# A fused decoder block: sums of the turned input on GpSimd, bias transfers and the fourth conv tile at other places

## The chip, the cores and the metric

The kernel runs on one core of a Trainium2 chip. A core has five engines that run their own instruction streams and wait for each other by semaphores: TensorE (PE, matmuls, with its weight loads PEld), VectorE (DVE), ScalarE (ACT), GpSimd (POOL) and SyncE (SP, here an issuer of DMA transfers). Matmuls write into PSUM, the other data lies in SBUF; both have 128 partitions. The metric is the time of one execution on the device in microseconds (us), lower is better.

## The reference

One decoder layer over 1024 tokens of width 1024, in fp32 throughout. A normalised input feeds one wide projection, whose columns are q, k, v, u and g. Two mixers work side by side, differential attention over q, k, v and a causal depthwise convolution of width 31 over a gated u; their results are merged by gates and projected, and a feed-forward part follows.

```python
h = rms_norm(x, attn_norm_w)
q, k, v, u, g = split(h @ w_in)                  # 1024, 1024, 1024, 2048, 2048 columns
q, k = rms_norm(q, q_norm_w), rms_norm(k, k_norm_w)      # per head half of 64
s = q_i @ k_i.T * 64**-0.5 + bias[rel]           # 8 heads, i = 1, 2; causal
a = (softmax(s_1) - lam * softmax(s_2)) @ v
y_a = rms_norm(a, subln_w) * (1 - lam_init) @ w_proj_attn
u_a, u_b = split(u)
c = causal_conv31(u_a * sigmoid(u_b), conv_w) + conv_b
y_b = silu(layer_norm(c)) @ w_proj_conv
g_a, g_b = split(sigmoid(g + gate_b))
x = x + (g_a * y_a + g_b * y_b) @ w_out
gt, up = split(rms_norm(x, ffn_norm_w) @ w_gate_up)
out = x + (silu(gt) * up) @ w_down
```

`bias[rel]` is a table of 32 buckets by 8 heads, looked up by the distance of query and key.

## The kernel before, in words

An fp32 matmul is made of three matmuls of a shorter type. Each operand is split into a high part (`hi`, a rounding cast on ScalarE, `split_hi`, L120) and a low part (`lo`, the operand less its high part, on VectorE, `split_lo`, L125, or on GpSimd, L131, while `low_by_pool` is set), and hi by hi, lo by hi and hi by lo are summed in PSUM (L168 to L170, and L944 in the products of the U stage).

The first stage is written as a generator. It yields a few dozen times, and the loop around it, at the bottom of the kernel, counts the yields in `n` and places background work at them. Its parts, in order:

- The opening (to 66.6 us). The 1024 tokens are normalised 128 at a time (`norm`, its last step L695 on VectorE) and turned by TensorE (L705, into PSUM as `px`) into `hT_hi` and `hT_lo`, the transposed input in two parts. Between the turns stand the first matmuls of V0 and of the first half of u. The steps are written in an order that is kept.
- The V stage: V1 and V2, two items of 256 columns of v, each in four steps of 48 matmuls, 256 wide. While they run, GpSimd, VectorE and ScalarE make the sums of the turned input that the next part needs.
- The U stage: u in seven pairs of column blocks (`u_pair`, c = 1 to 7). A pair is computed with seven products of 12 matmuls, 512 wide, in place of eight (a Strassen form over a 2 x 2 split of the contraction and of the tokens). The operands on the side of the input, T1 to T4, are sums of quarters F of the input; they are made once, in `sums_of_h`: F = hi + lo (`add`, on GpSimd, two instructions of 128x1024 for each quarter), differences of quarters (`less` and `less4`, on VectorE), and their high and low parts (`parts`, low on GpSimd, L890). The operands on the side of the weights are sums made for each pair in `prepare` (`s12`, `s34`, on GpSimd, L926 to L929), with their splits and that of the block 22 (`sh`, `sl`).
- Q0 and V3 (`run(last)`), and then the attention, whose first scores are L1243.

`tsum` is the list of the steps of `sums_of_h`; three are taken at each step of the V stage. `ws.fetch` loads weights ahead.

Two kinds of work run beside it. The convolution is 31 taps on VectorE for each of eight channel tiles (L580; ScalarE does the first tap, L574). Four tiles sum in a PSUM buffer of which there is one, so a tile ends with a copy to SBUF by ScalarE (`done`, L584) before the next begins; all four must be through before the attention takes that PSUM space. `bg` holds the taps as a list, `bg.step` issues some at each yield (2.75 on average), and `bg.until` issues what is due at a point. The bias is made by `bias_rows` at n = 18, 19, 20 (one matmul each, a copy by ScalarE into a `u2` tile, a transfer `b_d` on GpSimd's queue) and `bias_skew`, eight transfers on GpSimd's queue that spread a row over 128 partitions (`t_d<-b_d`, 576 KB each), one for each head.

Instructions are placed by a scheduler on their engine's stream in an order that may differ from that of the code, except where `after(...)` or `in_order` binds them; each engine and each DMA queue then runs its stream in order.

## Time and profile before

| | us |
|---|---|
| median of 3 runs | 1770.57 |
| lowest, highest | 1767.92, 1772.21 |
| the profiled execution | 1767.17 |
| its span | 1765.4 |
| TensorE busy | 1735.8 (98% of the span) |
| VectorE busy | 1267.4 (72%) |
| ScalarE busy | 856.5 (49%) |
| GpSimd busy | 198.7 (11%) |
| mean granted clock of TensorE | 0.994 of full speed |

The span is what lies between the first and the last instruction of the profiled execution. "Busy" counts the time in which an engine worked on an instruction; waiting is not in it. GpSimd's work lies almost all in the first stage. A row of the timeline has the start, the duration, the engine, the line, the operation, output and inputs by their names, the tile's shape, a count, and in brackets the idle time ahead of it with what ended that (`[2.29 <-DVE u L125]`: 2.29 us idle, released by VectorE's line 125). A row of a group has count, busy time and mean ns of one, and the idle time ahead. L12 is line 12 of the kernel before.

### The profile page before, as it was taken

How to read it: one execution, taken by the hardware profiler on the slowest of the kernel's cores; microseconds unless marked ns; L12 is line 12 of the kernel's file. 1: busy time of each engine (PE TensorE's matmuls, PEld its weight loads, DVE VectorE, ACT ScalarE, POOL GpSimd, SP SyncE). 2: the span in 40 equal slices, each digit the busy share in tenths (PEclk: the TensorE clock that was granted, in tenths of full speed). 3: DMA queues.
4: the chain of work that ended last, by engine and by line, in shares of the span. 5: the costliest groups of instructions: out<-in, count | busy, mean ns of one | idle time of the engine just before them, and what ended most of it. 6: DMA issues, size and time to landing. Idle time of an engine off the chain costs nothing.

```text
span 1765.4 us, 25829 instructions
## 1 busy us (share of the span) xinstructions
PE 1735.8 (98%) x9293; PEld 1493.0 (85%) x9293; DVE 1267.4 (72%) x2098; ACT 856.5 (49%) x1952; POOL 198.7 (11%) x190
## 2 busy tenths in 40 slices
PE   9989999999999999999999999999999999999999
PEld 7987789899998998987788788888888888888887
DVE  7696687799888988979678534877667666565544
ACT  5233335667776776755457313643333333333332
POOL 2696771000000000000000000000000000000000
PEclk9999999999999999999999999999999999999999
DMA  6235434433443433334773444234554544498663
GB/s 203 84 126 182 133 96 138 138 91 108 126 120 97 143 102 120 116 106 127 273 269 121 161 169 147 90 102 143 165 163 153 172 154 148 163 344 304 214 216 131
DMA packets 253253, 271.68 MB, mean 154 GB/s; under 512 B 15746, under 2 KB 177602, under 8 KB 253124
## 3 DMA queue, kind: packets, MB, share of 16 engines
q1 hardware_dynamic: 250848, 263.25, 46.0%
q0 software_dynamic: 1840, 5.19, 1.1%
q8 instruction: 73, 1.20, 0.3%
q10 hardware_dynamic: 436, 1.58, 0.2%
q14 instruction: 56, 0.46, 0.1%
HBM read 175.55 MB, written 78.16 MB: 144 GB/s over the span
## 4 chain that ended last, share of the span: by engine, by line
PE 88%; DVE 4%; ACT 2%; DMA 2%; POOL 2%; issue 1%; SPq 0%; ACTq 0%; DVEq 0%; POOLq 0%
PE acc L944 29%; PE acc L498 12%; PE pg L168 10%; PE pg L169 10%; PE pg L170 10%; PE sc L1243 2%; PE sc L1244 2%; PE pT L1282 2%; PE wo L168 2%; PE wo L170 2%; PE wo L169 2%; POOL F L864 1%; PE pW L169 1%; PE pW L168 1%; PE pW L170 1%
## 5 line engine op out<-in xcount | busy, mean ns | idle before, releaser
L580 DVE SCALAR_TENSOR_TENSOR acc<-u,cw,acc 128x1023 f32<-128x1023 f32 (+14 forms) x240 | 303.8, 1266 | 7.9 <-ACT acc L574 4.8
L168 PE MATMUL pg<-whi,hT_hi 128*128 128x256 f32 x704 | 200.7, 287 | 5.2 <-DVE u L125 3.7
L169 PE MATMUL pg<-wlo,hT_hi 128*128 128x256 f32 x704 | 201.5, 287 | 0.7 <-POOL wlo L131 0.7
L170 PE MATMUL pg<-whi,hT_lo 128*128 128x256 f32 x704 | 201.2, 286 | 0.0
L120 ACT CAST whi<-wraw 128x1024 fp32r<-128x1024 f32 x100 | 105.0, 1051 | 125.9 <-PE wo L170 48.1
L125 DVE TENSOR_TENSOR wlo<-draw,whi 128x1024 fp32r<-128x1024 f32 x75 | 91.7, 1223 | 82.7 <-ACT whi L120 79.5
L125 DVE TENSOR_TENSOR wlo<-wraw,whi 128x1024 fp32r<-128x1024 f32 x85 | 104.2, 1226 | 59.3 <-ACT whi L120 58.8
L168 PEld LDWEIGHTS pg<-whi,hT_hi 128*128 128x128 f32 x704 | 135.7, 193 | 7.8 <-DVE u L125 4.1
L120 ACT CAST whi<-draw 128x1024 fp32r<-128x1024 f32 x75 | 79.1, 1055 | 129.5 <-PE acc L498 116.0
L169 PEld LDWEIGHTS pg<-wlo,hT_hi 128*128 128x128 f32 x704 | 135.9, 193 | 2.5 <-POOL wlo L131 0.9
L170 PEld LDWEIGHTS pg<-whi,hT_lo 128*128 128x128 f32 x704 | 136.0, 193 | 1.6
L498 PE MATMUL acc<-wlo,whi 128*128 128x512 f32 x308 | 119.8, 389 | 0.0
L498 PE MATMUL acc<-whi,wlo 128*128 128x512 f32 x308 | 119.8, 389 | 0.0
L1250 ACT ACTIVATE E<-E,mn 128x640 f32<-128x640 f32 (+7 forms) x128 | 99.7, 779 | 30.8 <-DVE mn L1245 28.9
L168 PE MATMUL pg<-hT_hi,whi 128*128 128x512 f32 x288 | 114.2, 396 | 0.0
L169 PE MATMUL pg<-hT_lo,whi 128*128 128x512 f32 x288 | 114.1, 396 | 0.0
L170 PE MATMUL pg<-hT_hi,wlo 128*128 128x512 f32 x288 | 113.6, 394 | 0.0
L120 ACT CAST whi<-s 128x1024 fp32r<-128x1024 f32 x54 | 56.8, 1052 | 98.5 <-PE acc L944 83.0
L1245 DVE CUSTOM_DVE_ANT_0 E<-sc,tb 128x512 f32<-128x512 f32 (+3 forms) x128 | 74.5, 586 | 26.8 <-PE pT L1282 11.9
L944 PE MATMUL acc<-h_hi,whi 128*128 128x512 f32 x240 | 93.4, 389 | 0.0
L944 PE MATMUL acc<-h_lo,whi 128*128 128x512 f32 x240 | 93.4, 389 | 0.0
L944 PE MATMUL acc<-h_hi,wlo 128*128 128x512 f32 x240 | 90.1, 389 | 0.0
(336 smaller groups left out, 4559.1 us busy)
## 6 DMA issues: line engine op xcount, KB each, us to landing
wraw<-in_w_gate_up_dram SPq DMA_DIRECT2D x44, 512.0 KB, 4.8
wraw<-in_w_in_dram SPq DMA_DIRECT2D x40, 512.0 KB, 4.1
qs<-qs SPq DMA_DIRECT2D x96, 128.0 KB, 2.3
wd<-in_w_down_dram SPq DMA_DIRECT2D x44, 256.0 KB, 3.1
tdT<-wd SPq DMA_DIRECT2D x88, 128.0 KB, 4.8
draw<-sdS SPq DMA_DIRECT2D x44, 256.0 KB, 4.0
draw<-tdT SPq DMA_DIRECT2D x44, 256.0 KB, 3.9
wraw<-in_w_in_dram SPq DMA_DIRECT2D x32, 256.0 KB, 3.4
```

The lines of the kernel that those rows point to most:

```text
L120: act.copy(dst, src)
L125: last_lo[0] = dve.tensor_tensor(dst, src, f32(hi), op=ALU.subtract).ins
L168: pe.matmul(o, lh, rh, start=start, stop=False)
L169: pe.matmul(o, lh, rl, start=False, stop=False)
L170: last_mm[0] = pe.matmul(o, ll, rh, start=False, stop=stop).ins
L498: m = pe.matmul(o[s_][i][:], l_[:, ts], r_[:, 512:], start=start and j + y_ == 0, stop=j == n - 1 and y_ == 2, skip_group_check=not start,)
L580: dve.scalar_tensor_tensor(a_, us[c][:, : S - n], cw[:, c, t : t + 1], a_, op0=ALU.mult, op1=ALU.add)
L944: last_mm[0] = pe.matmul(o[:], a_[x_][:, k, :], b_[y_][:, k, :], start=start and k + x_ + y_ == 0, stop=k == 3 and x_ == 1, skip_group_che ...
L1243: pe.matmul(o[:, :w], qh[:, qs], k, start=True, stop=False)
L1244: last_mm[0] = pe.matmul(o[:, :w], ql[:, qs], k, start=False, stop=True).ins
L1245: dve.tensor_tensor_reduce(e[:, ks], o[:, :w], tb[:, S - nk + c0 : S - nk + c0 + w], 1.0, mn[:, j : j + 1] if c0 else 3.0e38, ALU.add, ALU ...
L1250: act.activation(e[:, :nk], e[:, :nk], AF.Exp, bias=mn[:, j : j + 1], scale=-1.0, accum_out=l[:, j : j + 1])
```

## The change

It has four parts.

1. The sums of the turned input. The quarters F get a pool of their own (`ff`), which exists from the kernel's start, so the first two of the four sums (f11, f21) are issued in the opening after `norm(7)` and the other two (f12, f22) after `v_tile(5)`. `less` and `less4` go from VectorE to GpSimd. What remains in `tsum` is taken one entry at each of the first five steps of the V stage, the rest at the sixth. The fetch of the first pair's weights comes one step later, and for the first pair `prepare` splits the first block ahead of the weight sums.
2. Block 22 (`sh`, `sl`) gets two buffers in place of one. To make room, `u2` has one buffer in place of two, and the V items' result tiles are `p1` and `u3` in place of `p1` and `u2`.
3. The eight bias transfers are issued at every third yield from n = 23, each bound behind the last GpSimd instruction issued by then; before, at every second yield from n = 24, unbound.
4. Taps come at 3.25 a yield in place of 2.75, and the `bg.until` that ends the fourth conv tile stands between the two items of `last` in place of behind the stage.

```diff
+    ff_ctx = ExitStack()
+    ff = ff_ctx.enter_context(tc.tile_pool(name="ff", bufs=1, reuse_waits="tile"))
...
     def half(tag):
-        return f32(st[0].tile([P, 512], F32R, tag=tag, name=nm(tag), bufs=2)[:])
+        return f32(st[0].tile([P, 512], F32R, tag=tag, name=nm(tag), bufs=1 if tag == "u2" else 2)[:])
+
+    adds = []
...
         def room(tag, dt, name):
-            return tt[0].tile([P, 4, 512], dt, tag=tag, name=name)
+            return (ff if tag[0] == "x" else tt[0]).tile([P, 4, 512], dt, tag=tag, name=name)
...
         def less(o, a_, b_):
             def go():
                 for e in two:
-                    dve.tensor_tensor(*[F[x_][:, e, :] for x_ in (o, a_, b_)], op=ALU.subtract)
+                    pool.tensor_tensor(*[F[x_][:, e, :] for x_ in (o, a_, b_)], op=ALU.subtract)
...
         def less4():
             for e, t_ in zip(two, ("s12", "s34")):
                 d = st[0].tile([P, 2, 512], F32, tag=t_, name=nm("T4"), bufs=1)
-                dve.tensor_tensor(d[:], F[f21][:, e, :], F[f22][:, e, :], op=ALU.subtract)
+                pool.tensor_tensor(d[:], F[f21][:, e, :], F[f22][:, e, :], op=ALU.subtract)
                 fourth.append(d[:])
...
         f11, f12, f21, f22 = (0, 0), (0, 1), (1, 0), (1, 1)
+        adds.extend([add(*f11), add(*f21), add(*f12), add(*f22)])
         return [
-            add(*f11), add(*f12), less(f11, f12, f11), add(*f22), less(f12, f22, f12), less(f22, f22, f11),
-            parts(2, ("y0", "y1"), halves(f22), pool), add(*f21), parts(1, ("y2", "y3"), halves(f11), pool), less4,
-            parts(3, ("x00", "x11"), halves(f12), pool), parts(4, ("x01", "x10"), None, pool),
+            less(f11, f12, f11), less(f12, f22, f12), less(f22, f22, f11),
+            parts(2, ("y0", "y1"), halves(f22), pool), parts(1, ("y2", "y3"), halves(f11), pool),
+            less4, parts(3, ("x00", "x11"), halves(f12), pool), parts(4, ("x01", "x10"), None, pool),
         ]
...
-    def prepare(w, cols, s_pool, s_bufs=1):
+    def prepare(w, cols, s_pool, s_bufs=2, sums_later=False):
...
         for n, _ in enumerate(run(first)):
-            for _ in range(3):
-                if tsum:
-                    tsum.pop(0)()
-            if n == 1:
+            if n < 5:
+                tsum.pop(0)()
+            if n == 2:
                 ws.ahead = 1
                 ws.fetch()
                 ws.ahead = 0
             if n == 4:
                 next(ups[0])
+                A = next(ups[0])
             if n == 5:
-                A = next(ups[0])
+                while tsum:
+                    tsum.pop(0)()
...
             ws.ahead = 2
-            yield from run(last)
+            yield from run(last[:1])
+            bg.until((NKT - CONV_PSUM) * (CW + 1) - 1)
+            yield from run(last[1:])
...
             lambda: norm(7),
         )
+        adds.pop(0)()
+        adds.pop(0)()
...
             lambda: v_tile(5),
         )
+        adds.pop(0)()
+        adds.pop(0)()
...
-        v_tiles[0] = tiles_from(st[0], ("p1", "u2"))
+        v_tiles[0] = tiles_from(st[0], ("p1", "u3"))
...
-        if n >= 24 and n % 2 == 0 and (n - 24) // 2 < H:
-            bias_skew((n - 24) // 2)
-        due += 2.75
+        if n >= 23 and n % 3 == 2 and (n - 23) // 3 < H:
+            with after(last_of(mybir.EngineType.Pool)):
+                bias_skew((n - 23) // 3)
+        due += 3.25
...
-    bg.until((NKT - CONV_PSUM) * (CW + 1) - 1)
```

How it moves instructions, at three places. The first is GpSimd from the opening into the V stage. F_962 to F_965 are the four quarters, T1l and T2l low parts of sums, wlo_1094 and wlo_1100 the low halves of V2's two weight blocks. Before:

```order
L746 DMA rb<-in_rel_bias_dram 32x8
L864 TENSOR_TENSOR F_962<-hT_hi,hT_lo 128x1024 x2
L864 TENSOR_TENSOR F_963<-hT_hi,hT_lo 128x1024 x2
L864 TENSOR_TENSOR F_964<-hT_hi,hT_lo 128x1024 x2
L864 TENSOR_TENSOR F_965<-hT_hi,hT_lo 128x1024 x2
L131 TENSOR_TENSOR wlo_1094<-wraw_1091,whi_1093 128x1024
L890 TENSOR_TENSOR T1l<-F_962,T1h 128x1024 x2
L890 TENSOR_TENSOR T2l<-F_964,T2h 128x1024 x2
L131 TENSOR_TENSOR wlo_1100<-wraw_1097,whi_1099 128x1024
```

After, where F_320, F_323, F_321, F_322 are f11, f21, f12, f22, T_118 and T_119 the two halves of the fourth sum, and wlo_1158 and wlo_1164 V2's low halves:

```order
L868 TENSOR_TENSOR F_320<-hT_hi,hT_lo 128x1024 x2
L868 TENSOR_TENSOR F_323<-hT_hi,hT_lo 128x1024 x2
L868 TENSOR_TENSOR F_321<-hT_hi,hT_lo 128x1024 x2
L868 TENSOR_TENSOR F_322<-hT_hi,hT_lo 128x1024 x2
L877 TENSOR_TENSOR F_320<-F_321,F_320 128x1024 x2
```

and right behind them:

```order
L877 TENSOR_TENSOR F_321<-F_322,F_321 128x1024
L894 TENSOR_TENSOR T1l<-F_320,T1h 128x1024
L877 TENSOR_TENSOR F_321<-F_322,F_321 128x1024
L894 TENSOR_TENSOR T1l<-F_320,T1h 128x1024
L877 TENSOR_TENSOR F_322<-F_322,F_320 128x1024
L131 TENSOR_TENSOR wlo_1158<-wraw_1155,whi_1157 128x1024
L877 TENSOR_TENSOR F_322<-F_322,F_320 128x1024
L884 TENSOR_TENSOR T_118_1364<-F_323,F_322 128x1024
L894 TENSOR_TENSOR T2l<-F_322,T2h 128x1024
L884 TENSOR_TENSOR T_119_1366<-F_323,F_322 128x1024
L894 TENSOR_TENSOR T2l<-F_322,T2h 128x1024
L131 TENSOR_TENSOR wlo_1164<-wraw_1161,whi_1163 128x1024
```

The differences L877 and L884, which were on VectorE, stand now ahead of and between the low parts, and V2's second low half comes behind all of them.

The second place is GpSimd in the U stage around the bias transfers (t_d_300 to t_d_307 before, t_d_303 to t_d_310 after; s_ are weight sums, u_ a part of u's result). Before:

```order
L927 TENSOR_TENSOR s_162_1703<-s_162_1703,wraw_1668 128x512
L756 DMA t_d_300<-b_d 128x1152
L756 DMA t_d_301<-b_d 128x1152
L756 DMA t_d_302<-b_d 128x1152
L756 DMA t_d_303<-b_d 128x1152
L756 DMA t_d_304<-b_d 128x1152
L756 DMA t_d_305<-b_d 128x1152
L756 DMA t_d_306<-b_d 128x1152
L756 DMA t_d_307<-b_d 128x1152
L929 TENSOR_TENSOR s_163_1704<-wraw_1668,s_162_1703 128x512
```

After:

```order
L758 DMA t_d_304<-b_d 128x1152
L131 TENSOR_TENSOR wlo_2001<-wraw_1963,whi_2000 128x1024
L935 TENSOR_TENSOR s_202_1999<-wraw_1963,wraw_1965 128x512
L936 TENSOR_TENSOR s_202_1999<-wraw_1963,s_201_1998 128x512
L131 TENSOR_TENSOR sl_2104<-wraw_1965,sh_2103 128x512
L131 TENSOR_TENSOR wlo_2044<-s_201_1998,whi_2043 128x1024
L758 DMA t_d_305<-b_d 128x1152
L933 TENSOR_TENSOR s_219_2145<-wraw_2112 128x512
L934 TENSOR_TENSOR s_219_2145<-s_219_2145,wraw_2110 128x512
L989 TENSOR_TENSOR u_206_2041<-u_206_2041,u_205_2027 128x512
L131 TENSOR_TENSOR wlo_2100<-s_202_1999,whi_2099 128x1024
```

The eight transfers stood in one block, and now they stand one to twelve rows of other work apart.

The third place is ScalarE ahead of the first scores, where `done` is the copy that ends the fourth conv tile, qkraw and jk are Q1's evictions and squares, and vh is V3's last eviction. Before:

```order
L777 COPY qkraw_3181<-pg_3183 128x512
L780 ACTIVATE jk_3233,ss_323_3182<-pg_3183 128x64 x8
L777 COPY qkraw_3181<-pg_3270 128x512
L780 ACTIVATE jk_3320,ss_323_3182<-pg_3270 128x64 x8
L630 ACT_TABLE_LOAD
L630 ACTIVATE t_3332<-v_3329 128x16
L631 ACT_TABLE_LOAD
L631 ACTIVATE r_3331<-t_3332 128x16
L777 COPY qkraw_3385<-pg_3387 128x512
L584 COPY done_3121<-acc_2512 128x1024
```

After:

```order
L120 CAST whi_2873<-wraw_2870 128x1024
L120 CAST vh_3133<-pg_3084 128x512
L1351 ACT_TABLE_LOAD
L277 ACTIVATE lsum<-lsum 128x2
L120 CAST whi_3190<-wraw_3188 128x1024
L586 COPY done_2860<-acc_2397 128x1024
L779 COPY qkraw_3200<-pg_3202 128x512
L782 ACTIVATE jk_3252,ss_323_3201<-pg_3202 128x64 x8
```

The copy stood behind Q1's first half and its norm's two tables, and now stands ahead of Q1's first eviction, one table load and one weight cast behind V3's last eviction.

More of the change, by code (lines that the diff above doesn't have):

```diff
@@ L924, in prepare @@
         A["11"], A["12"] = parts(*[t_[:] for t_ in wsplit(raws[0])])
+        if sums_later:
+            yield A
         eng = pool if low_by_pool[0] else dve
@@ L929, in prepare @@
         eng.tensor_tensor(s34[:, 512:1024], a12, s12[:, 512:1024], op=ALU.subtract)
-        yield A
+        if not sums_later:
+            yield A
         A["S1"], A["S2"] = parts(*[t_[:] for t_ in wsplit(s12)])
@@ L996, in first_stage @@
         nonlocal qkp
+        tsum = sums_of_h()
         yield from opening()
-        tsum = sums_of_h()
-        ups = [prepare(win, (U0 + D + c * P, U0 + c * P), st[0]) for c in range(1, NKT)]
+        ups = [prepare(win, (U0 + D + c * P, U0 + c * P), st[0], 2, c == 1) for c in range(1, NKT)]
         def weights_ahead():
@@ L1027, in first_stage @@
         tt_ctx.close()
+        ff_ctx.close()
         qkp = qk_ctx.enter_context(tc.tile_pool(name="qkp", bufs=2, side="right", reuse_waits="tile"))
```

## The prediction

> **What bounds the kernel now.** I read the profile's page first: the busy time of the engines and, in its part 4, the chain of work that ended last.
>
> ```profile
> PE 1735.8 (98%) x9293; PEld 1493.0 (85%) x9293; DVE 1267.4 (72%) x2098; ACT 856.5 (49%) x1952; POOL 198.7 (11%) x190
> PE 88%; DVE 4%; ACT 2%; DMA 2%; POOL 2%; issue 1%; SPq 0%; ACTq 0%; DVEq 0%; POOLq 0%
> ```
>
> TensorE bounds the whole run, so the change can only win what TensorE loses: its idle time, and the time in which it runs at half clock after an idle stretch. The change touches the first 340 us, and the windows there show where that is. A row has the window, its length, then busy time and instruction count of PE, PEld, DVE, ACT and POOL, the granted clock, and DMA.
>
> ```profile
> 66.60:91.20 24.60, 24.60 (x205) 24.42 (x203) 22.98 (x10) 7.88 (x9) 24.60 (x9) 1.00 0.25 86
> 91.20:104.70 13.50, 8.29 (x44) 7.60 (x44) 13.36 (x13) 4.37 (x5) 13.50 (x6) 0.75 0.31 103
> 121.50:176.40 54.90, 54.65 (x233) 42.17 (x232) 37.54 (x36) 19.91 (x28) 41.26 (x34) 1.00 0.55 173
> 176.40:186.20 9.80, 5.76 (x14) 4.52 (x15) 3.18 (x3) 1.53 (x2) 5.74 (x4) 0.65 0.53 174
> 331.00:340.00 9.00, 5.96 (x25) 5.35 (x25) 5.07 (x16) 7.33 (x22) 0.00 (x0) 0.62 0.32 117
> ```
>
> Three windows have a clock under 1. The timeline's rows of the matmuls that end the waits say who was late (in brackets: idle time ahead, and what ended it):
>
> ```profile
> 93.52 0.38 PE L168 MATMUL pg<-whi,hT_hi 128*128 128x256 f32 x1 [2.29 <-DVE u L125]
> 96.91 0.79 PE L168 MATMUL pg<-whi,hT_hi 128*128 128x256 f32 x2 [1.52 <-ACT whi L120]
> 102.55 0.39 PE L168 MATMUL pg<-whi,hT_hi 128*128 128x256 f32 x1 [1.39 <-DVE u L125]
> ...
> 180.44 0.80 PE L944 MATMUL acc<-hT_hi,whi 128*128 128x512 f32 x1 [4.04 <-ACT whi L120]
> ...
> 334.13 0.80 PE L1243 MATMUL sc<-ks,qs 128*128 128x512 f32 x1 [3.04 <-ACT done L584]
> ```
>
> V stage: the undisturbed window gives 24.60/205 = 0.12 us for a matmul, so the 44 of the next need 5.3 of its 13.50: 8.2 lost, 5.2 of it idle and the rest half clock. U stage (176.4): 4.04 idle, and 5.76 busy at half clock, half of it lost: 6.9. Attention start (331): 3.04 idle and by the same count 2.8 of half clock: 5.9. At most 21.0 us are to be had. A spell of half clock is (1 - 0.62) x 9.0/0.5 = 6.8 us long and costs up to 3.4.
>
> **Opening: the first sums run beside it.** Four additions now start as soon as the fourth block of tokens is turned, where VectorE's chain of the norm sets TensorE's turns.
>
> ```profile
> 22.45 0.51 POOL L746 DMA_DIRECT2D rb<-in_rel_bias_dram  x1
> 60.05 2.40 POOL L864 TENSOR_TENSOR F<-hT_hi,hT_lo 128x1024 f32<-128x1024 f32 x1 [37.09 <-DMA v_lo<-vl]
> ...
> 312.68 2.39 POOL L131 TENSOR_TENSOR wlo<-wraw,whi 128x1024 fp32r<-128x1024 f32 x1 [19.42 <-ACT whi L120]
> 314.51 1.64 DVE L125 TENSOR_TENSOR wlo<-wraw,whi 128x1024 fp32r<-128x1024 f32 x1 [0.26 <-ACT whi L120]
> ...
> 23.89 1.29 DVE L125 TENSOR_TENSOR hT_lo<-px,hT_hi 128x512 fp32r<-128x512 f32 x2 [1.08 <-ACT hT_hi L120]
> 25.81 1.23 DVE L125 TENSOR_TENSOR wlo<-wraw,whi 128x1024 fp32r<-128x1024 f32 x1
> 28.67 0.16 DVE L635 TENSOR_TENSOR t<-r 128x2 f32<-128x2 f32 x1
> 29.27 0.16 DVE L638 TENSOR_TENSOR r<-r,t 128x2 f32<-128x2 f32 x1
> 29.46 2.74 DVE L695 SCALAR_TENSOR_TENSOR xt<-xt,r,anw_b 128x512 f32<-128x512 f32 x4
> 46.45 1.29 DVE L125 TENSOR_TENSOR hT_lo<-px,hT_hi 128x512 fp32r<-128x512 f32 x2 [2.46 <-ACT hT_hi L120]
> ...
> 32.80 1.03 PE L705 MATMUL px<-ident,xt 128*128 128x128 f32 x8
> 37.60 1.25 PE L705 MATMUL px<-ident,xt 128*128 128x128 f32 x8 [1.03 <-DVE hT_lo L125]
> ```
>
> An addition of 128x1024 takes 2.40. The wlo pair shows what it does to VectorE: VectorE's wlo began at 314.51 while GpSimd's ran until 312.68 + 2.39 = 315.07, and ended 1.08 after that, 1.64 long where it takes 1.23 alone (row 25.81). I read from it that the two exclude each other, one instruction at a time, when VectorE's has both inputs in SBUF. GpSimd is free from 22.96. The first addition can start when the first of the two hT_lo ends, about 24.6, and then they alternate: addition to 27.0, wlo to 28.1, addition to 30.5, L635, addition to 33.0, L636, addition to 35.4, L638, and L695 begins near 35.3 where it began at 29.46: +5.85. TensorE's turn at 32.80 then waits to about 36.7 (3.9 idle, inside that delay), and the turn at 37.60, which waits for VectorE already, comes 5.9 later, with 0.2 for half clock: +6.1. Bounds: 0, if GpSimd starts late or VectorE's small operations slip between; and, if each of four operations waits out a whole addition, 4 x 2.40 = 9.6, with 3.4 of half clock, +13.0. I take the worked chain, which stands on rows of this place. The two later sums stand beside operations that read PSUM (hT_lo from px), which show no exclusion, and cost nothing there; otherwise the upper bound has them.
>
> **V stage: the other sums move to GpSimd.** Two groups of VectorE in 66 to 122 us and a row of GpSimd:
>
> ```profile
> L873 DVE TENSOR_TENSOR F<-F,F 128x1024 f32<-128x1024 f32 x6 | 17.9, 3004 | 4.7 <-POOL F L864 4.7
> L880 DVE TENSOR_TENSOR T<-F,F 128x1024 f32<-128x1024 f32 x2 | 5.0, 2500 | 0.0
> ...
> 90.56 3.33 POOL L890 TENSOR_TENSOR T1l<-F,T1h 128x1024 fp32r<-128x1024 f32 x1
> ```
>
> These 17.9 + 5.0 = 22.9 us leave VectorE, which was busy 13.36 of 13.50 where the stall is; what stays there (taps, low halves of pg) reads PSUM. GpSimd gets 8 more operations. The last one that V2 needs is the low half of its second weight block (wlo_1164), the 18th from the third sum on. The third sum waits for the last turned block (row 46.45: first half done 47.1), with the delay of the opening 53.2; 18 x 2.40 = 43.2 gives 96.4. TensorE starts V2 at 66.6 + 6.1 + 192 x 0.12 = 95.7, and 46 matmuls, 5.6, stand ahead of that operand: 101.3. Slack 4.9, so no stall: -8.2. Bounds: -8.2, and 0 if a wait stays.
>
> A rule of the Trainium skill speaks against this part ("Perfetto Trace Analysis", Optimizing Scalar/DVE Operations): GpSimd and VectorE share an SBUF read port, so offloading between those two might not help. By that rule the term would be 0 and the sum -5.8. Row 314.51 agrees on the exclusion; that VectorE's remaining work here reads PSUM is why I don't take the result.
>
> **U stage: bias transfers spread.**
>
> ```profile
> 179.34 1.04 ACT L120 CAST whi<-wraw 128x1024 fp32r<-128x1024 f32 x1 [7.26 <-DMA wraw<-in_w_in_dram]
> 158.38 4.12 POOL L756 DMA_DIRECT2D t_d<-b_d  x8 [0.41 <-issue]
> ...
> t_d<-b_d POOLq DMA_DIRECT2D x8, 576.0 KB, 10.8
> ```
>
> All eight transfers are issued from 158.38 within 4.12 us, 4.6 MB in flight together, and ScalarE's cast waits 7.26 for its weight. Now one to twelve GpSimd operations stand between two of them, so one or two are in flight: the stall goes, -6.9 (bounds -6.9 and 0: even a single one may delay a weight). GpSimd's queue is held 4.12/8 = 0.5 us at a time in place of 4.1 at once; it is busy 41.26 of 54.90, and only sums and low halves of the next pair are queued behind. Two buffers for block 22, one for u2 and the later fetch change how early such work may be; it is done about a pair (7 products of 12 matmuls) ahead, so I cost them at nothing; with that cover gone, the 2.40 of one low half would show.
>
> More taps (3.25 a step in place of 2.75) are VectorE work that comes earlier, and its waits for TensorE in 121.5 to 256 cover it:
>
> ```profile
> L580 DVE SCALAR_TENSOR_TENSOR acc<-u,cw,acc 128x1004 f32<-128x1004 f32 (+14 forms) x64 | 81.3, 1270 | 5.8 <-ACT acc L574 4.2
> L985 DVE TENSOR_TENSOR p<-acc,p 128x512 f32<-128x512 f32 x6 | 4.2, 692 | 8.4 <-PE acc L944 8.3
> L979 DVE TENSOR_TENSOR u<-acc,u 128x512 f32<-128x512 f32 x6 | 4.1, 690 | 14.2 <-PE acc L944 14.2
> ```
>
> 64 taps x (3.25/2.75 - 1) = 11.6 more, x 1.27 = 14.8 us, against 8.3 + 14.2 = 22.5 idle.
>
> **Attention start.** The last tap and its eviction were late:
>
> ```profile
> 328.62 1.28 ACT L630 ACT_TABLE_LOAD   x1
> 331.56 0.57 ACT L777 COPY qkraw<-pg 128x512 f32<-128x512 f32 x1
> ...
> 331.69 0.17 DVE L635 TENSOR_TENSOR t<-r 128x16 f32<-128x16 f32 x1 [1.72 <-ACT r L631]
> ...
> 333.06 1.01 ACT L584 COPY done<-acc 128x1024 f32<-128x1024 f32 x1 [0.93 <-DVE acc L580]
> ```
>
> The tap stood behind the norm, and that waited for ScalarE's tables. Now behind V3's last matmul come the eviction vh 0.57, a table load 1.28, the small lsum 0.2, whi 1.04, wlo 1.23, two taps 2.5 and `done` 1.01: 7.8, with some 0.1 between each two 8.4. TensorE has 85 matmuls from there to its first scores, 10.2. Slack 1.8. I take -5.0 of 5.9 (bounds -5.9 and 0), since the slack is small against a chain of seven steps.
>
> **Sum:** +6.1 - 8.2 - 6.9 - 5.0 = -14.0. The profiled execution took 1767.17 (span 1765.4, 1.8 around it): 1753.2. It lies 3.4 below the median of the runs, 1770.57, so I forecast 1770.57 - 14.0 = 1756.6.
>
> The clock's price has a rule as well: the Trainium skill ("TensorE: Matmul & The Clock Gate", Part 1, The HAM clock gate) has the clock halved after at least one idle window of about 3.4 us. By it the V stage's waits, 2.29 the longest, would cost only their 5.2, and the sum would be -11.0; the window at 91.2 shows 0.75 after 2.29, so the measured 8.2 stands.
>
> **Rivals.** (A) The sum above.
> (B) The opening costs nothing, its lower bound: -20.1, 1750.5. For it: no row shows the two engines together there for more than an instant. Against: the pair at 314.51.
> (C) Work shifted between two engines that exclude each other gains nothing in the V stage, and the rest holds: 6.1 - 6.9 - 5.0 = -5.8, 1764.8. For it: GpSimd is busy all of 66.6 to 104.7 already. Against: two of the three late operands are VectorE's, which gets 22.9 us back. A stall that stays in the U stage instead gives nearly the same, -7.1.
> (D) The other side: GpSimd becomes the bound of V2. If its operations take the 3.33 of the contended row 90.56 and the opening its upper bound, the third sum starts at 47.1 + 13.0 = 60.1, wlo_1164 ends 18 x 3.33 = 59.9 later at 120.0, and is needed at 108.2: a wait of 11.8, and 3.4 of half clock. Sum 13.0 - 8.2 + 15.2 - 6.9 - 5.0 = +8.1, 1778.7. It decides from a mean operation of 2.88: 60.1 + 18 x 2.88 - 108.2 = 3.7 of wait, which with 3.4 eats the 7.1 left. For it: 3.33 in the stage itself. Against: what made it long there, L873 and L880 on VectorE, is what leaves.
> (E) The opening at its upper bound and C together: 13.0 - 6.9 - 5.0 = +1.1, 1771.7: no change.
>
> **Numbers.** A 0.48, B 0.15, C 0.14, E 0.08, D 0.15. A's own range is 1750 to 1762. For 8 in 10 the range takes in B below (1746: -21.0, and 3.4 for the scatter of the runs) and E above (1772), and leaves D out. About 0.2%, 3.5 us, is what a measurement of this kernel can tell from no change: faster A, B, C 0.77; same E 0.08; slower D 0.15.
>
> **What would show it.** V stage: no wait of TensorE from 66 to 125 us, and no F<-F on VectorE; wrong, if a low half by GpSimd ends a wait there. Opening: L695 of the third pair of blocks near 35, and V1 at 72.7. U stage: t_d landing well under 10.8 and no half clock near 180. Attention start: the first scores released by something other than `done`. The forecast fails if the first scores come less than 10 us earlier than at 334.13, or if TensorE waits in the U stage for evictions that stand behind the added taps on VectorE.

## The result, and the profile after

| | us |
|---|---|
| before, median of 4 runs (lowest, highest) | 1769.59 (1767.92, 1772.21) |
| changed, median of 4 runs (lowest, highest) | 1749.57 (1747.49, 1750.50) |
| ratio, 95% interval | 0.9884, 0.9867 to 0.9901 |
| profiled executions, before and changed | 1767.17 and 1750.50 |

The changed kernel is 20.0 us faster by the medians and 16.7 by the two profiled executions. The forecast was 1756.6, 14.0 faster, with a range of 1746 to 1772. The profile's page of the changed kernel, the same two rows as before:

```profile
PE 1730.0 (99%) x9293; PEld 1490.4 (85%) x9293; DVE 1255.9 (72%) x2090; ACT 854.4 (49%) x1950; POOL 212.2 (12%) x198
PE 92%; DVE 3%; DMA 2%; ACT 1%; issue 1%; SPq 0%; DVEq 0%; ACTq 0%
```

The windows of the changed kernel that answer to those of before (columns as there). The first two are the opening, the next the V stage, the U stage, and the start of the attention:

```profile
33.20:36.60 3.40, 0.00 (x0) 0.03 (x1) 3.29 (x5) 0.41 (x2) 2.10 (x1) 1.00 0.01 3
36.60:46.00 9.40, 7.56 (x33) 6.05 (x34) 8.18 (x19) 4.23 (x7) 0.00 (x0) 0.82 0.08 29
72.89:128.00 55.11, 55.11 (x425) 53.56 (x424) 40.26 (x38) 20.23 (x25) 51.96 (x27) 1.00 0.40 130
128.00:258.00 130.00, 130.00 (x576) 105.25 (x576) 94.97 (x89) 50.23 (x67) 97.94 (x67) 1.00 0.43 139
310.00:325.00 15.00, 12.75 (x87) 12.13 (x86) 4.07 (x16) 8.16 (x32) 0.00 (x0) 0.89 0.81 249
```

TensorE has no idle time and full clock from 72.89 to 258, so the V and U stages' losses are gone. The opening has a new one, and the start of the attention still has one. The timeline's rows for the opening, VectorE first, then GpSimd, then TensorE:

```profile
26.04 2.35 DVE L125 TENSOR_TENSOR wlo<-wraw,whi 128x1024 fp32r<-128x1024 f32 x1
28.31 2.35 DVE L665 TENSOR_SCALAR v<-ssx 128x2 f32<-128x2 f32 x1
31.14 1.88 DVE L637 TENSOR_TENSOR t<-r 128x2 f32<-128x2 f32 x1
33.05 2.26 DVE L638 SCALAR_TENSOR_TENSOR t<-v,t 128x2 f32<-128x2 f32 x1
35.75 2.74 DVE L697 SCALAR_TENSOR_TENSOR xt<-xt,r,anw_b 128x512 f32<-128x512 f32 x4
...
53.50 9.46 POOL L868 TENSOR_TENSOR F<-hT_hi,hT_lo 128x1024 f32<-128x1024 f32 x4 [18.21 <-DVE hT_lo L125]
95.80 2.41 POOL L131 TENSOR_TENSOR wlo<-wraw,whi 128x1024 fp32r<-128x1024 f32 x1 [0.15 <-ACT whi L120]
...
36.61 1.85 PE L707 MATMUL px<-ident,xt 128*128 128x128 f32 x8 [3.41 <-issue]
72.89 0.28 PE L168 MATMUL pg<-whi,hT_hi 128*128 128x256 f32 x1
```

Lines of the changed kernel are two higher here: L665, L637, L638 and L697 are L663, L635, L636 and L695 of before. wlo and three operations on 2 columns that took under 0.2 take some 2 us each, L697 begins at 35.75, and V1 at 72.89 in place of 66.60. The start of the attention, ScalarE, VectorE, SyncE's queue and TensorE:

```profile
310.42 1.01 ACT L586 COPY done<-acc 128x1024 f32<-128x1024 f32 x1 [3.75 <-DVE acc L582]
...
319.08 0.69 DVE L1261 CUSTOM_DVE_ANT_0 E<-sc,tb 128x512 f32<-128x512 f32 x1 [8.69 <-DMA tb<-t_d]
...
309.05 0.58 SPq L1229 DMA_DIRECT2D vh<-v_hi  x1
311.02 1.47 SPq L1229 DMA_DIRECT2D vl<-v_lo  x1
312.53 1.45 SPq L1238 DMA_DIRECT2D tb<-t_d  x1
...
319.83 0.33 PE L1259 MATMUL sc<-ks,qs 128*128 128x128 f32 x1 [2.25 <-DVE mn L1261]
```

`done` no longer ends a wait of TensorE. The first scores begin at 313.76, and then VectorE cannot evict them until head 0's bias table `tb` has landed, whose load stands on SyncE's queue behind the two loads of head 0's v.

Head 7 of the attention is a place that the change doesn't touch in the code. The same 75 us up to the last scores, before and after:

```profile
760.00:835.00 75.00, 70.78 (x394) 59.91 (x393) 63.05 (x133) 43.91 (x115) 1.81 (x10) 1.00 0.38 113
```

```profile
743.00:818.00 75.00, 75.00 (x420) 64.41 (x419) 63.05 (x134) 46.79 (x118) 1.87 (x10) 1.00 0.39 117
```

TensorE lost 4.2 us there before and loses nothing now.

### The profile page after: what moved, and what is told of

It reads as the page before. It is cut to its first block, busy times and chain, and to the rows that moved or that the text cites. A ratio compares the mean times of both kernels' runs of the same rounds, so it can differ in the third digit from the quotient of the medians.

```text
span 1748.7 us, 25856 instructions
## 1 busy us (share of the span) xinstructions
PE 1730.0 (99%) x9293; PEld 1490.4 (85%) x9293; DVE 1255.9 (72%) x2090; ACT 854.4 (49%) x1950; POOL 212.2 (12%) x198
## 4 chain that ended last, share of the span: by engine, by line
PE 92%; DVE 3%; DMA 2%; ACT 1%; issue 1%; SPq 0%; DVEq 0%; ACTq 0%
PE acc L952 29%; PE acc L500 12%; PE pg L168 11%; PE pg L170 11%; PE pg L169 11%; PE sc L1260 2%; PE sc L1259 2%; PE pT L1298 2%; PE wo L170 2%; PE wo L169 2%; PE wo L168 2%; PE pW L168 1%; PE pW L169 1%; PE pW L170 1%; PE pg L1072 1%; DMA gt<-g_d 1%
```

## The experiments

Every run was timed beside the kernel before on the same chip; its median lay between 1768.9 and 1769.6 in all of them, so medians are compared with 1749.57 of the changed kernel as they stand. Twelve kernels ran.

### The opening: the first sums held back

```diff
             lambda: norm(7),
         )
-        adds.pop(0)()
-        adds.pop(0)()
+        gate = ff.tile([P, 8], F32, tag="gate", name="gate")
+        with after(pool.tensor_copy(gate[:, :1], xts[7][:, D - 1 : D]).ins):
+            adds.pop(0)()
+            adds.pop(0)()
```

> The changed kernel, with the first two sums of the opening (four additions on GpSimd) held back until the last norm of the opening is done on VectorE, by a one-element copy on GpSimd that reads what that norm wrote. If the 6.3 us that V1 starts later (72.89 in place of 66.60) come from VectorE and GpSimd excluding each other in the opening's norm, V1 starts again at 66.6 and the kernel is 6.3 us faster than the changed one, about 1743.3, with no wait in the V stage: the four additions take 9.6 us from about 37 and end at 46.8, just ahead of the last turned block. If the opening is longer for another reason (GpSimd's queue, the transfers), V1 stays near 72.9 and the time near 1749.6. If the four additions were needed as early as that, a wait of up to 5 us for a low half appears in V2 and the gain is under 2 us.

1742.92 us (1742.15 to 1744.43), ratio to before 0.9853 (0.9837 to 0.9870): 6.7 us faster than the changed kernel, and, with the other kernel that holds them back (below), the fastest of all that ran. Its timeline, GpSimd, VectorE and TensorE, and its window of V1 and V2:

```profile
37.04 0.19 POOL L1146 COPY gate<-xt 128x1 f32<-128x1 f32 x1 [11.32 <-DVE xt L697]
37.19 9.43 POOL L868 TENSOR_TENSOR F<-hT_hi,hT_lo 128x1024 f32<-128x1024 f32 x4
47.23 9.46 POOL L868 TENSOR_TENSOR F<-hT_hi,hT_lo 128x1024 f32<-128x1024 f32 x4 [0.62 <-DVE hT_lo L125]
...
25.83 1.23 DVE L125 TENSOR_TENSOR wlo<-wraw,whi 128x1024 fp32r<-128x1024 f32 x1
28.70 0.16 DVE L637 TENSOR_TENSOR t<-r 128x2 f32<-128x2 f32 x1
...
66.65 0.28 PE L168 MATMUL pg<-whi,hT_hi 128*128 128x256 f32 x1
```

```profile
66.60:121.50 54.90, 54.90 (x424) 53.25 (x424) 40.03 (x37) 20.15 (x25) 51.77 (x26) 1.00 0.41 130
```

With the additions behind the last norm, wlo and the 2-column operations have their old lengths, V1 starts at 66.65, and the V stage has no wait. So the price of the opening is the overlap of the four additions with the norm, and holding them back costs nothing later: they end at 46.6, and the next pair can't start before 47.23 in any case.

### The V stage: the differences back on VectorE

```diff
-                    pool.tensor_tensor(*[F[x_][:, e, :] for x_ in (o, a_, b_)], op=ALU.subtract)
+                    dve.tensor_tensor(*[F[x_][:, e, :] for x_ in (o, a_, b_)], op=ALU.subtract)
...
-                pool.tensor_tensor(d[:], F[f21][:, e, :], F[f22][:, e, :], op=ALU.subtract)
+                dve.tensor_tensor(d[:], F[f21][:, e, :], F[f22][:, e, :], op=ALU.subtract)
```

> The changed kernel with the differences (less, less4: 8 operations) back on VectorE, the additions still early in the opening. If the V stage's waits came from VectorE's 22.9 us in contention, they return: 5 to 8 us slower than the changed kernel, about 1756, with L873-like operations near 3.0 us each. If it is the early additions alone that cleared the V stage, there is no wait there and the time stays within 2 us of 1749.6; by the rule that shifting work between the two engines might not help, it stays there too.

1754.50 us (1754.19 to 1758.37), ratio 0.9920 (0.9906 to 0.9934): 4.9 slower than the changed kernel. Rows of its timeline, GpSimd, VectorE and TensorE:

```profile
75.50 6.64 POOL L894 TENSOR_TENSOR T1l<-F,T1h 128x1024 fp32r<-128x1024 f32 x2
...
76.55 3.35 DVE L125 TENSOR_TENSOR wlo<-wraw,whi 128x1024 fp32r<-128x1024 f32 x1
...
79.95 0.58 PE L169 MATMUL pg<-wlo,hT_hi 128*128 128x256 f32 x1 [4.91 <-DVE wlo L125]
```

There is one wait, not three, and its form is another than I expected: with the additions early, six of the eight differences run at 1.21 (the other two take 3.4 and 3.3), but V1's second low half stands behind them on VectorE and then loses to GpSimd's T1l (3.35 for 1.23). With the additions early in both kernels, the move of the differences was worth 4.9 us, against the rule of the Trainium skill ("Perfetto Trace Analysis", Optimizing Scalar/DVE Operations) that such a move might not help. What the early additions are worth in the V stage by themselves no run shows: none has them late and the differences on GpSimd.

### The U stage: the block of transfers, or the buffer of block 22

Four kernels bear on it. First, the changed kernel with the transfers in one block, and the kernel before with them spread:

```diff
-        if n >= 23 and n % 3 == 2 and (n - 23) // 3 < H:
-            with after(last_of(mybir.EngineType.Pool)):
-                bias_skew((n - 23) // 3)
+        if n >= 24 and n % 2 == 0 and (n - 24) // 2 < H:
+            bias_skew((n - 24) // 2)
```

> The changed kernel with the eight bias transfers issued as before, in one block. If the block is the cause of the U stage's wait for a weight, a wait of about 4 us with half clock behind it returns, 6.9 us slower: about 1756.5, with the eight landing at about 10.8 us each. If the wait was an accident of where the weights' fetches stood, nothing returns and the time stays at 1749.6.

1753.84 us (1752.31 to 1754.89), ratio 0.9912 (0.9897 to 0.9926): 4.3 slower. But not in the U stage. Its window there, its eight transfers and the fetch of the next pair's weights:

```profile
128.00:258.00 130.00, 130.00 (x576) 105.31 (x575) 99.39 (x92) 49.97 (x67) 98.16 (x69) 1.00 0.46 147
```

```profile
160.26 4.14 POOL L758 DMA_DIRECT2D t_d<-b_d  x8 [0.40 <-issue]
...
147.63 5.06 SPq L916 DMA_DIRECT2D wraw<-in_w_in_dram  x2
```

The block is there, and no wait: both blocks of weights were requested by 152.7, ahead of it. In the kernel before one was requested at 163.84, with the block in flight since 158.38, and ScalarE's cast could use it at 179.34. Two rows of the chain that led to the wait there (the second from the view of the chain, with the time to the landing):

```profile
162.51 1.31 POOL L929 TENSOR_TENSOR s<-wraw,s 128x512 f32<-128x512 f32 x1
...
163.84 15.47 DMA wraw<-in_w_in_dram
```

The block acts twice in that chain. Its eight issues hold GpSimd's queue until 162.50, L929 stands behind them, and L929 is the last reader of the buffer into which the next weights go, so these are requested as soon as it ends. Then the load takes 15.47 us beside the eight transfers, the last of which lands 16.7 us after its issue at 161.99; where no block is in flight, the six loads of this line in 119 to 200 us that the trace times took 3.6 to 4.7.

The rest of the kernel has another order in the attention (1102 projection matmuls ahead of the first scores in place of 1141); which of its waits make up the 4.3 us is left open.

The other way round, the spread in the kernel before (the same lines, exchanged):

> The kernel before with the bias transfers spread (part 3 alone). With the other parts in, the block of transfers did not bring the U stage's wait back, so two theories are left. If the block was the cause in the kernel before, and there alone because its weights were fetched at that moment, the wait of 4.04 us and its half clock go: 6.9 us faster than before, about 1762.5. If the wait came from the weights' own place (one buffer for block 22, the later V stage), it stays near 176 and the time stays within 2 us of 1769.5.

1765.49 us (1763.40 to 1770.00, 12 runs), ratio 0.9983 (0.9972 to 0.9994): 3.4 faster, half of the term. Its rows, TensorE, ScalarE and GpSimd:

```profile
192.10 0.79 PE L944 MATMUL acc<-T2h,wlo 128*128 128x512 f32 x1 [3.00 <-POOL wlo L131]
...
174.62 0.62 ACT L120 CAST sh<-wraw 128x512 fp32r<-128x512 f32 x1 [2.09 <-PE acc L944]
...
182.86 1.30 POOL L926 TENSOR_TENSOR s<-wraw 128x512 f32<-128x512 f32 x1 [5.73 <-DMA wraw<-in_w_in_dram]
```

The wait of 4.04 is gone: the load that goes out at 160.87, as soon as L929 ends, takes 3.7 us. So the block was the cause of that wait. But 12 us later one of 3.00 is there. Followed back: TensorE waits for a low half of a weight sum, GpSimd's sums wait 5.73 for weights, and these were requested late, at 176.64, since the cast of block 22 (`sh`) waits for the product that still reads its one buffer, and holds the weights' buffer until then. The load then takes 6.08 us, with a bias transfer issued at 176.55, just ahead of it. So I undid the buffers in the changed kernel:

```diff
-        return f32(st[0].tile([P, 512], F32R, tag=tag, name=nm(tag), bufs=1 if tag == "u2" else 2)[:])
+        return f32(st[0].tile([P, 512], F32R, tag=tag, name=nm(tag), bufs=2)[:])
...
-    def prepare(w, cols, s_pool, s_bufs=2, sums_later=False):
+    def prepare(w, cols, s_pool, s_bufs=1, sums_later=False):
...
-        ups = [prepare(win, (U0 + D + c * P, U0 + c * P), st[0], 2, c == 1) for c in range(1, NKT)]
+        ups = [prepare(win, (U0 + D + c * P, U0 + c * P), st[0], 1, c == 1) for c in range(1, NKT)]
...
-        v_tiles[0] = tiles_from(st[0], ("p1", "u3"))
+        v_tiles[0] = tiles_from(st[0], ("p1", "u2"))
```

> The changed kernel with part 2 undone: one buffer for block 22, two for u2, the V items' tiles p1 and u2. With the transfers spread in the kernel before, the wait at 176 went, but one of 3.00 us came at 189 for a weight sum's low half, whose weights were fetched late: the cast of block 22 waited for the product that still read its only buffer, and the weights' buffer was held for that long. If the buffer is the cause, a wait of 3 us with half clock returns in the U stage: 3 to 5 us slower than the changed kernel, about 1753.5. If the V stage's relief is what keeps the weights early, the time stays at 1749.6, as the forecast's cost of nothing has it.

1757.90 us (1755.76 to 1760.33), ratio 0.9932 (0.9919 to 0.9946): 8.3 slower than the changed kernel. The same wait, with the same chain, though the transfers are spread (the last two rows are a bias transfer and the request of the late weights):

```profile
188.84 0.53 PE L952 MATMUL acc<-T2h,wlo 128*128 128x512 f32 x1 [2.69 <-POOL wlo L131]
...
171.46 0.62 ACT L120 CAST sh<-wraw 128x512 fp32r<-128x512 f32 x1 [1.91 <-PE acc L952]
...
179.59 1.30 POOL L933 TENSOR_TENSOR s<-wraw 128x512 f32<-128x512 f32 x1 [5.62 <-DMA wraw<-in_w_in_dram]
...
173.39 0.58 POOL L758 DMA_DIRECT2D t_d<-b_d  x1
...
173.47 0.38 SPq L916 DMA_DIRECT2D wraw<-in_w_in_dram  x1
```

With the second buffer gone the wait is back, so that buffer is what keeps it away in the changed kernel. It need not be the whole of the wait: here too a single bias transfer goes out just ahead of the late request, and the load takes 5.99 us, where the one at 158.52 took 3.8. The 2.2 us between the two are most of the 2.69, but no run has the late load without a bias transfer beside it. Some 4.4 of the 8.3 us lie in the U stage by the trace (2.69 and 1.7 of half clock); 2.6 more are two waits in the attention (1.20 at 574 and 1.38 at 705), whose order moved with it.

Last, the first two parts alone, with the block and the old taps:

```diff
-            yield from run(last[:1])
-            bg.until((NKT - CONV_PSUM) * (CW + 1) - 1)
-            yield from run(last[1:])
+            yield from run(last)
...
-        if n >= 23 and n % 3 == 2 and (n - 23) // 3 < H:
-            with after(last_of(mybir.EngineType.Pool)):
-                bias_skew((n - 23) // 3)
-        due += 3.25
+        if n >= 24 and n % 2 == 0 and (n - 24) // 2 < H:
+            bias_skew((n - 24) // 2)
+        due += 2.75
...
+    bg.until((NKT - CONV_PSUM) * (CW + 1) - 1)
     low_by_pool[0] = False
```

> Parts 1 and 2 alone (the sums on GpSimd, begun in the opening, and the buffers), with the transfers in one block and the taps as before. By the measured terms, 6.3 for the opening and -8.2 for the V stage, with the U stage's 6.9 gone through the second buffer of block 22: 9 us faster than before, about 1760. If the U stage's wait belongs to the block, it stays here and the gain is about 2 us: 1767.

1760.37 us (1758.66 to 1761.74), ratio 0.9947 (0.9933 to 0.9961): 9.2 faster than before, as the sum +6.3 - 8.2 - 6.9 = -8.8 has it. The U stage's 6.9 us are gone without the spread: the block goes out at 161.31, and both blocks of weights were requested by 155.1, ahead of it. No kernel has part 1 and the block with one buffer, so what part 1 does for this is not shown. In its attention it is the kernel before again:

```profile
326.21 0.50 PE L1257 MATMUL sc<-ks,qs 128*128 128x512 f32 x1 [3.04 <-ACT done L586]
770.51 0.47 PE L1257 MATMUL sc<-ks,qs 128*128 128x512 f32 x1 [1.50 <-DMA ks<-klo]
```

### The taps: their rate, or the place where the fourth tile ends

The part undone in the changed kernel (2.75 a step, `bg.until` behind the stage, as in the last diff without the transfers):

> The changed kernel with the taps as before (2.75 a step, the fourth tile ended behind the stage). In the changed kernel the wait ahead of the scores is no longer for the tile's copy but for the bias table of head 0, 2.25 us with some half clock, so the part gained about 2.5 us by the trace and not the 5.0 forecast: by that, 2 to 3 us slower than the changed kernel, about 1752. If the 5.0 were right, 1754.6. If the four waits of head 7 in the kernel before (4.2 us between 777 and 826) also came from the later taps, they return and it is 6 to 7 us slower, about 1756.

1759.64 us (1757.10 to 1761.25), ratio 0.9944 (0.9930 to 0.9958): 10.1 slower, more than any theory said. And the part alone in the kernel before:

> The kernel before with the taps' part alone (3.25 a step, the fourth tile ended between the last two items). Undone in the changed kernel this part cost 10.1 us, of which the trace shows 4.6 us as waits in the attention and less at its start. If that is its worth by itself, 8 to 10 us faster than before, about 1760.5, with the wait for the tile's copy and the waits of 777 to 826 gone. If its worth hangs on the relieved VectorE of the V stage (the added taps are 14.8 us of work there), the added taps lengthen the V stage's waits and the gain is under 5 us. By the forecast's term, 5.0: 1764.5.

1755.84 us (1754.90 to 1758.82), ratio 0.9926 (0.9913 to 0.9938): 13.1 faster than before, although its V stage keeps the three waits (2.30, 2.03, 1.28) and its U stage has two (1.81 and 2.52 near 190). The wait of 4.04 is not there: L929 stands ahead of the block in this order, the weights are requested at 160.20 and land after 3.6 us; it is the next load, requested at 175.49, that takes 8.46 us beside the block and ends in the wait of 2.52. The part I had priced at 5.0 is the largest. Its two halves apart, first the rate alone:

```diff
-        due += 3.25
+        due += 2.75
```

> The changed kernel with 2.75 taps a step, the end of the fourth tile kept between the last two items. In eight kernels the waits of head 7 in the attention (4 to 6 us) are there when the first scores stand behind all of Q1's matmuls ahead of them (1200 projection matmuls) and gone when they stand behind fewer (1064 to 1141), which leaves 120 rather than 97 of them to head 7. If the place of the tile's end sets this, the rate is worth nothing: within 2 us of 1749.6. If the rate sets it, the waits return: about 1757.

1757.05 us (1755.12 to 1759.26), ratio 0.9928 (0.9916 to 0.9941): 7.5 slower. The theory I favoured, the place, falls. The waits are not in head 7 this time, but earlier in the attention:

```profile
383.40 0.47 PE L1259 MATMUL sc<-ks,qs 128*128 128x512 f32 x1 [1.59 <-DMA ks<-klo]
387.00 0.39 PE L168 MATMUL pg<-whi,hT_hi 128*128 128x256 f32 x1 [1.28 <-ACT jk L782]
...
400.90 0.39 PE L168 MATMUL pg<-whi,hT_hi 128*128 128x256 f32 x1 [1.92 <-ACT jk L782]
```

Then the place alone:

```diff
-            yield from run(last[:1])
-            bg.until((NKT - CONV_PSUM) * (CW + 1) - 1)
-            yield from run(last[1:])
+            yield from run(last)
...
+    bg.until((NKT - CONV_PSUM) * (CW + 1) - 1)
     low_by_pool[0] = False
```

> The changed kernel with 3.25 taps a step and the fourth tile ended behind the stage as before. If the place of the tile's end sets the attention's waits: 1200 projection matmuls ahead of the first scores and about 1758. If the rate alone has the taps through by then, the tile ends early by itself and nothing changes: 1749.6.

1750.26 us (1747.98 to 1751.55), ratio 0.9888 (0.9874 to 0.9901): 0.7 slower, no difference that can be told. So it is the rate that counts; with the old rate the place is worth at most 2.6 us (1759.64 against 1757.05, medians whose runs overlap). What the traces show of how it acts: in the nine kernels with 3.25 that ran, 1064 to 1141 projection matmuls (into `pg`) stand ahead of the first scores, in the five with 2.75 there are 1200. The matmuls that are not spent there fill the attention; in head 7 there are 120 of them in the changed kernel and 96 in the kernel before, which is most of the difference between the two windows of 75 us above (420 and 394 instructions). This is not the rate's doing alone: 96 stand in head 7, with 3.6 to 4.4 us of waits, only in the four kernels that have both the rate and the place of before. The one with the old rate alone has 118 there and no wait, and loses its 7.5 us elsewhere, by the three waits above and the half clock behind the last (0.57 from 402 to 406). VectorE's taps go the same way: by the first scores 120 are done in every kernel, but head 0 takes 21 in place of 9, and head 7 12 in place of 13. That the scheduler lets the attention begin earlier because the fourth tile is through earlier is my reading of this; no run holds the order fixed and moves the taps alone, and the kernel with one buffer for block 22, which has 3.25, has waits in its attention too. So that the rate costs 7.5 us is shown, and why it does is not.

### The start of the attention: the bias table first

```diff
     inatt[0] = True
+    load_bias(0)
     load_v(0)
...
-        if n % NT == 0:
+        if n % NT == 0 and n:
             load_bias(h)
```

> The changed kernel with the load of head 0's bias table issued ahead of the two loads of head 0's v. If the wait of 2.25 us in the first scores is for that table (VectorE waits 8.69 us for it), it goes with its half clock: 2 to 4 us faster than the changed kernel, about 1746.5. If the transfers are limited by the load on the DMA engines there (0.81 busy in 310 to 325), the table lands as late or v comes late in its place: no change, 1749.6.

1749.89 us (1748.49 to 1750.91), ratio 0.9890 (0.9875 to 0.9904): no change. The table came in time, and TensorE waits a little later, nearly as long (1.82 for 2.25), for ScalarE's squares of Q1:

```profile
327.00 0.39 PE L168 MATMUL pg<-whi,hT_hi 128*128 128x256 f32 x1 [1.82 <-ACT jk L782]
```

Together with the sums held back:

> Both edits together: the first two sums held back until the opening's last norm, and head 0's bias table loaded ahead of v. If they are independent, the gain of the held-back sums (1742.9) and a wait of 1.42 us less: about 1741.3. If the table's place gains nothing, 1742.9.

1744.02 us (1741.41 to 1747.09), ratio 0.9858 (0.9841 to 0.9874): the same as the held-back sums alone within what can be told, with the same wait for the squares, 1.34. The kernel to keep is the one with the sums held back.

## Where the prediction held, and where not

The direction is right, and the time lies within the range of 1746 to 1772, though just below A's own of 1750 to 1762; the gain is 20.0 us and not 14.0. That the sum came as near as it did is in part luck: the U stage's 6.9 came out with the help of a part that was costed at nothing, and the 3.0 us that are missing at the attention's start are made up for by 4.2 in head 7 that were not forecast. Term by term:

- Opening, +6.1: V1 starts 6.3 later. L695 was forecast at 35.3 (35.75 measured) and TensorE's turn at 36.7 (36.61), and holding the additions back returned 6.7. Four operations of VectorE were held, as forecast, but one of them was another: L663 and not L638. Rival B, the opening at nothing, ends nearest to the measured time (1750.5), and is refuted all the same: its reason didn't happen.
- V stage, -8.2: right, no wait. The third sum starts at 53.50 (53.2 forecast), and wlo_1164 ends at 98.2 (96.4), which leaves 3.4 of the 4.9 us of slack. Rivals C, D and E are out: the 18 operations of GpSimd take 44.7 us, 2.48 each, not the 3.33 of D nor the 2.88 from which it would have decided, and the move gains.
- U stage, -6.9: the time is right, and the block was the cause of the wait of before, as forecast; the transfers land in 5.4 us in place of 10.8. But "one or two in flight" was not enough: the spread gained 3.4 by itself, with a new wait 12 us later. The step that failed is the second buffer of block 22, costed at nothing: in the kernels that have it neither wait is there, with the spread or with the block. I had read the row of the wait for `wraw` as a slow transfer, which it was (15.47 us), and didn't ask why it was asked for no earlier than 163.84. Its buffer was freed by L929, behind the block on GpSimd's queue, and the 4.1 us for which the block holds that queue were counted as harmless.
- Attention start, -5.0: some -2.0. `done` ends at 311.43, 7.9 behind V3's last matmul (8.4 forecast), and the wait for it goes; but I named nothing that is late next, and that is the bias table, 2.25 us with some 1.7 of half clock behind it (5.9 - 3.9 = 2.0). The first scores come 20.4 us earlier (313.76 for 334.13); some 7 of these are the 59 projection matmuls, at 0.12 each, that now stand behind them.
- The taps, 0: this is the largest miss. "Its waits for TensorE cover it" is right as a cost, but the whole part, forecast at the 5.0 of the attention's start, is worth 10.1 when it is undone and 13.1 alone, and the rate 7.5 of the 10.1. The gain comes with another order in the attention, which I treated as untouched; 4.2 us of it lie in head 7, by rate and place together.
- The rest of the difference between 14.0 and 20.0: by the two profiled executions the gain is 16.7, and 3.3 is that the profiled execution of before lay 2.4 below its median and that of the changed kernel 0.9 above. Of the 16.7, by the rows below, +6.3 lie ahead of V1, -24.1 between V1 and the projection behind the attention (873.94 - 66.60 = 807.3 before, 856.08 - 72.89 = 783.2 after), and +1.2 behind it, where the profiled execution of the changed kernel has some 1.7 of half clock that the other hasn't (last section). In the middle part V stage, U stage, attention start and head 7 make -8.2 - 6.9 - 2.0 - 4.2 = -21.3, two small waits of before that are gone (0.25 at 166, 0.66 at 314) another 0.9, and one of 0.70 at 396 is new; 2.6 stay unassigned. The parts don't add up: measured alone in the kernel before, the first two together gained 9.2, the third 3.4 and the fourth 13.1, in all 25.7 against 20.0.

```profile
873.94 0.50 PE L168 MATMUL pg<-aTh,whi 128*128 128x512 f32 x1 [2.90 <-DVE gt L1579]
```

```profile
856.08 0.80 PE L168 MATMUL pg<-aTh,whi 128*128 128x512 f32 x1 [2.90 <-DVE gt L1595]
```

## What to carry to other kernels

When a transfer ends a wait, look at when it was requested as well as at how long it took: here a slow load (15.47 us) had also been asked for late, and asking for it earlier was the remedy that left no wait behind. Background work that shares a scheduler with the main work is not priced by its own time alone; a change of its rate, and of where it must end, can go with another order of the main work, and with waits, far behind the place of the change. And before work is put beside a chain on VectorE, see whether the chain's operations read SBUF alone: here 9.6 us of GpSimd work held up four operations, three of them of under 0.2 us, and could wait 12 us (37.19 for 24.89) at no cost.

## What the runs showed of the hardware that was not expected

The half clock behind a gap is not settled by the gap's length. At the place of the last two rows TensorE waits 2.90 us in every kernel. In nine of the fourteen half clock follows and in five it does not; the changed kernel is one of the nine, the one with the sums held back one of the five (the window of 4 us behind the wait in the changed kernel, then row and window of the other):

```profile
856.00:860.00 4.00, 3.92 (x11) 3.11 (x12) 3.76 (x7) 2.33 (x5) 0.00 (x0) 0.58 0.84 258
```

```profile
849.03 0.50 PE L168 MATMUL pg<-aTh,whi 128*128 128x512 f32 x1 [2.90 <-DVE gt L1597]
...
849.00:853.00 4.00, 3.97 (x17) 3.30 (x18) 3.78 (x6) 2.28 (x5) 0.00 (x0) 1.00 0.83 255
```

The granted clock is 0.58 in the one and 1.00 in the other, which costs some 1.7 us. Spells of half clock were about 3.4 us long behind some waits (in the window 310 to 325 of the changed kernel, (1 - 0.89) x 15/0.5 = 3.3) and 6.8 behind others (the three of before). The Trainium skill ("TensorE: Matmul & The Clock Gate", Part 1, The HAM clock gate) has the clock watched in windows of about 3.4 us that run free of the kernel; the lengths seen, one or two such windows, and the same wait with and without a price agree with that, and its idle window of 3.4 us as the condition is more than the 2.25 that were enough here.

An operation with one input was held as well, which I had counted as free of the exclusion: L665 above, a scale and add on 128x2 in SBUF, 2.35 us beside an addition of GpSimd. The same operation on 128x1 was not, beside an operation of GpSimd, in the kernel before, and neither was the reciprocal on 128x2 (0.17 us at 30.93) beside an addition in the changed kernel (rows of the kernel before, GpSimd's row, then VectorE's):

```profile
10.89 2.39 POOL L1087 TENSOR_TENSOR vwl<-wraw,vwh 128x1024 fp32r<-128x1024 f32 x1 [9.58 <-ACT vwh L120]
...
12.37 0.15 DVE L663 TENSOR_SCALAR v<-ssx 128x1 f32<-128x1 f32 x1 [0.36 <-ACT xj L677]
```

The Trainium skill ("SBUF — State Buffer", SBUF: two separate sides) has VectorE contend for the port that it shares with GpSimd not only with two SBUF inputs but also in a 2-port perf mode. That would separate L665 from the other two if it ran in such a mode and they did not; no run here shows the mode.
